# Down-projection of a two-layer decoder trunk: partial sums over all feature pairs kept in PSUM, product by product

## The chip, the cores and the metric

The kernel runs on one core of a Trainium2 chip. The metric is the device time of one execution in microseconds (us), lower is better. A core has five instruction streams that the text names: PE (TensorE matmuls; its weight loads are listed as PEld), DVE (VectorE), ACT (ScalarE), POOL (GpSimd) and SP (SyncE, which here only issues DMAs). Each stream runs its instructions in the order in which the scheduler has written them; an instruction that waits holds up what stands behind it on its engine.

## The reference

The program is one inference step of a decoder trunk of two layers, over 1024 prompt tokens and 8 x 8 sample tokens, so 1088 token rows of 1024 numbers. Each layer is a mixer (a gated delta rule in layer 0, dilated window attention in layer 1) followed by a SwiGLU feed-forward; between the layers one key/value projection is made. The part that the change touches is the feed-forward with its residual:

```python
def swiglu(x, w_in, w_out):
    gate, up = jnp.split(x @ w_in, 2, axis=-1)
    return (jax.nn.silu(gate) * up) @ w_out
...
        x = x + rms_norm(swiglu(rms_norm(x, norms[layer, 2]), ffn_w_in[layer], ffn_w_out[layer]), norms[layer, 3])
```

The inner width is 2816, which is 22 feature tiles of 128 (NF = 22), or 11 pairs of them. All numbers are float32.

## The kernel before

Tokens come in nine tiles (TILES): 0 to 7 of 128 prompt tokens each and tile 8 with the 64 sample tokens. A float32 matmul is made of three matmuls of a reduced format: every operand is split into a rounded part (hi, made by ACT with a copy) and the rest (lo, made by a subtraction x - hi on DVE or POOL), and hi x hi, lo x hi and hi x lo are added up in PSUM.

Each layer runs `ffn_in` and then `ffn_out`. `ffn_in` is the up-projection: 11 blocks of two feature tiles, each a fast 2 x 2 matrix multiplication with seven products in place of eight. Its weight sums are made by POOL (L294), split by ACT and DVE (L303, L304), its gate products are made by POOL (L323), and at a block's end one POOL DMA (L357) writes the block's activations, a tile called `wide`, to a DRAM scratch `gd` of [22, 128, 1088].

`ffn_out` is the down-projection, again with seven products on a 2 x 2 split: tokens in two halves of 512 (tiles 0 to 3 and 4 to 7), output columns in two halves of 512, and the feature tiles of a pair as even and odd. It works through blocks of two feature pairs, five blocks, and within a block through the products j = 0 to 6. Each feature's activations (`graw`, 544 KB) and weights (`wraw`, 512 KB) are loaded by SP (L410, L412). For each product the token sums `s` and weight sums `t` are made on POOL (L428 to L439), both operands are split into `ga` and `wa` (hi at L379 on ACT, lo at L380 on DVE and POOL in the turn DVE, POOL, DVE), four token tiles of six matmuls of 512 columns each run on PE (L394), and each result is added from PSUM to an SBUF sum by DVE (L398; copied by ACT in the first block). Tile 8 is multiplied plainly with `gdec`, a split of its 64 columns. The 11th pair is done as a plain product, merged with the residuals tile by tile: `residual` squares on ACT, takes the root on POOL (L153, L154), scales and adds on DVE (L217, L218) and POOL (L216, L219). In layer 0 the same loop goes on, for each tile, to `scale`, `turn` (eight transposes, L187) and the key/value projection `kv_proj` (24 matmuls, L1289).

A scheduler sets the order of instructions on each engine. What it may hoist is limited by the ring sizes of the tile pools: `ga` and `wa` have four buffers each, `graw` and `wraw` eight.

Of the kernel before, what the change touches and what calls it, by code (L numbers as in the profile page):

```python
# [13 lines left out]
F32 = mybir.dt.float32  # L14
F32R = mybir.dt.float32r
# [7 lines left out]
P = 128  # L23
# [13 lines left out]
HALF = T // 2  # L37
# [42 lines left out]
class Net:  # L80
# [185 lines left out]
    def ffn_in(self, w_in, gd):  # L266
# [7 lines left out]
        with ExitStack() as es:  # L274
# [62 lines left out]
            for blk in range(NF // 2):  # L337
# [19 lines left out]
                nc.gpsimd.dma_start(gd[2 * blk:2 * blk + 2].rearrange("f p t -> p f t"), y.rearrange("p f x t -> p f (x t)"))  # L357

    def ffn_out(self, gd, w_out, grow_idx, xin, xout, after):
# [3 lines left out]
        nc, tc = self.nc, self.tc  # L363
        with ExitStack() as es:
# [3 lines left out]
            halves = cycle((nc.vector, nc.gpsimd, nc.vector))  # L368

            def main(raw, half):  # L370
                return bass.AP(tensor=raw.tensor, offset=raw.offset + half * HALF, ap=[list(raw.ap[0]), [HC[1][0], 2], [1, 256]])

            def split(pool, tag, x, bufs):
                t = pool.tile([P, 2, 512], F32R, tag=tag, name=tag, bufs=bufs)
                if len(x.shape) == 3:
                    hi, lo = (t[:, i].rearrange("p (c t) -> p c t", c=2) for i in range(2))
                else:
                    hi, lo = t[:, 0], t[:, 1]
                nc.scalar.activation(hi, x, AF.Copy)  # L379
                next(halves).tensor_sub(lo, x, hi)  # L380
                return t

            def decode(raw):
                t = fy.tile([P, 2 * SD], F32R, tag="gdec", name="gdec", bufs=4)
                hi, lo = (t[:, x * SD:x * SD + SD].rearrange("p (x t) -> p x t", x=2) for x in range(2))
                x = raw[:, :, 256:288]
                nc.scalar.activation(hi, x, AF.Copy)
                nc.vector.tensor_sub(lo, x, hi)
                return t

            def accumulate(out, seq, first=False):
                ps = self.bank("mm")
                for i, (a, b) in enumerate(seq):
                    nc.tensor.matmul(ps, a, b, start=i == 0, stop=i == len(seq) - 1)  # L394
                if first:
                    nc.scalar.activation(out, ps, AF.Copy)
                else:
                    nc.vector.tensor_add(out, out, ps)  # L398
# [1460 lines left out]
```

## Time and profile before

| | us |
|---|---|
| time before, median of 3 runs | 3381.87 (3379.75 to 3384.51) |
| the profiled execution's own time | 3379.78 |
| span of its profile | 3378.1 |
| first ffn_out (layer 0, with the key/value projection) | 1388.3 to 1740.3 |
| second ffn_out (layer 1), which ends the program | 3071.5 to 3378.1 |
| PE busy over the span | 3121.5 (92%) |
| DVE, ACT, POOL busy over the span | 2252.6 (67%), 1541.1 (46%), 1408.5 (42%) |

The profile gives busy time by engine for any stretch (windows), groups of equal instructions with their mean length and with what ended the idle time before them, and a timeline by engine, in which `[2.07 <-POOL ga L380]` behind a row says that the engine stood idle for 2.07 us before it and that a POOL instruction of line 380, which wrote a tile `ga`, ended the wait. The granted clock is the share of TensorE's full speed: 1.00 is 2.4 GHz and 0.50 is 1.2 GHz.

### The profile page before, as it was taken

The page shows a single profiled execution, that of the slowest core. Times are in us where ns is not written, and L with a number is a line of the kernel's source. Part 1 is how long each engine was busy: PE and PEld are TensorE (multiplying, and loading weights), DVE is VectorE, ACT ScalarE, POOL GpSimd, SP SyncE. Part 2 cuts the span into 40 slices and gives each one's busy share as a digit, 9 for nine tenths or more (in the row PEclk, how much of TensorE's full clock was granted, in tenths as well). Part 3 has the DMA queues.
Part 4 walks back from the last instruction along what each step waited for, and adds up shares of the span by engine and source line. Part 5 has one row for each costly group of instructions (what it writes and reads, how often), then busy time and mean ns, then how long its engine had stood idle before and what let it go on. Part 6 is the DMA issues. An engine that isn't in the chain of part 4 may idle for free.

```text
span 3378.1 us, 54405 instructions
## 1 busy us (share of the span) xinstructions
PE 3121.5 (92%) x20096; PEld 2847.5 (84%) x20096; DVE 2252.6 (67%) x4661; ACT 1541.1 (46%) x3783; POOL 1408.5 (42%) x1350
## 2 busy tenths in 40 slices
PE   7899999999899999899899999998898999998986
PEld 7888888888799999777689888887686999997774
DVE  5667777624665555688856777677656655556898
ACT  5445555434433333443457677766334333334333
POOL 3333333343454444487631213120123544445877
PEclk9999999999999999999899999999889999999998
DMA  4233333345322221421251112112442222214113
GB/s 143 92 99 100 111 106 99 98 124 183 109 75 75 77 76 63 149 91 65 96 158 47 32 54 60 32 47 68 157 125 97 77 77 77 77 65 168 67 62 113
DMA packets 248839, 311.80 MB, mean 92 GB/s; under 512 B 33058, under 2 KB 204306, under 8 KB 248572
## 3 DMA queue, kind: packets, MB, share of 16 engines
q1 hardware_dynamic: 240572, 276.20, 25.9%
q0 software_dynamic: 7856, 31.56, 2.3%
q8 instruction: 159, 2.61, 0.3%
q14 instruction: 108, 0.88, 0.1%
q10 hardware_dynamic: 144, 0.56, 0.0%
HBM read 227.91 MB, written 80.36 MB: 91 GB/s over the span
## 4 chain that ended last, share of the span: by engine, by line
PE 63%; DVE 14%; POOL 8%; ACT 6%; issue 6%; DMA 3%; SPq 0%; POOLq 0%; ACTq 0%; DVEq 0%
PE mm L355 27%; PE mm L394 6%; PE mm L764 5%; PE mm L1346 5%; PE mm L567 4%; PE B L1054 2%; PE mm L1289 1%; DVE yc L811 1%; ACT s L1437 1%; PE sc L1431 1%; PE o L1469 1%; DVE wa L380 1%; PE A L987 1%; PE tr L1450 1%; DVE qs L1357 1%
## 5 line engine op out<-in xcount | busy, mean ns | idle before, releaser
L394 PE MATMUL mm<-wa,ga 128*128 128x512 f32 x1872 | 472.6, 410 | 65.3 <-DVE wa L380 23.6
L394 PEld LDWEIGHTS mm<-wa,ga 128*128 128x128 f32 x1872 | 364.5, 197 | 167.2 <-DVE wa L380 34.1
L764 PE MATMUL mm<-h_hi,w 128*128 128x352 f32 (+1 forms) x1536 | 440.4, 345 | 10.3 <-ACT xr L801 8.1
L1346 PE MATMUL mm<-h_hi,w 128*128 128x352 f32 (+1 forms) x1152 | 354.4, 342 | 0.0
L764 PEld LDWEIGHTS mm<-h_hi,w 128*128 128x128 f32 x1536 | 280.1, 191 | 22.1 <-ACT xr L801 9.0
L323 POOL TENSOR_TENSOR wide<-wide,v 128x288 f32<-128x288 f32 (+1 forms) x176 | 162.4, 936 | 244.5 <-DVE v L322 244.5
L764 PE MATMUL mm<-h_lo,w 128*128 128x352 f32 (+1 forms) x768 | 257.6, 335 | 0.0
L304 DVE TENSOR_TENSOR s<-w,s 128x512 fp32r<-128x512 f32 x132 | 165.1, 1252 | 128.9 <-ACT s L303 128.6
L303 ACT ACTIVATE s<-t 128x512 fp32r<-128x512 f32 x176 | 111.1, 632 | 288.0 <-PE mm L355 277.6
L294 POOL TENSOR_TENSOR t<-w 128x512 f32<-128x512 f32 x88 | 114.6, 1304 | 299.0 <-issue 159.6
L1346 PEld LDWEIGHTS mm<-h_hi,w 128*128 128x128 f32 x1152 | 212.3, 189 | 1.6
L1437 ACT ACTIVATE s<-s,stat 128x128 f32<-128x128 f32 (+1 forms) x384 | 169.4, 442 | 93.4 <-DVE stat L1435 91.1
L145 POOL TENSOR_TENSOR w<-raw,w 128x1024 fp32r<-128x1024 f32 x38 | 100.5, 2645 | 240.8 <-ACT w L142 181.4
L1346 PE MATMUL mm<-h_lo,w 128*128 128x352 f32 (+1 forms) x576 | 189.3, 329 | 0.0
L567 PE MATMUL mm<-mw_hi,o_hl 128*128 128x512 f32 x544 | 177.3, 403 | 3.7 <-ACT o_hl L555 3.7
L1454 DVE TENSOR_TENSOR pl<-tr,ph 128x256 fp32r<-128x256 f32 (+1 forms) x192 | 104.6, 545 | 106.7 <-ACT ph L1453 105.7
L304 DVE TENSOR_TENSOR s<-t,s 128x512 fp32r<-128x512 f32 x176 | 131.6, 749 | 39.7 <-ACT s L303 39.4
L355 PE MATMUL mm<-b0h,s 128*128 128x256 f32 (+1 forms) x704 | 144.5, 292 | 12.2 <-ACT s L303 9.6
L811 DVE SCALAR_TENSOR_TENSOR yc<-xr,convw,yc 128x1112 f32<-128x1112 f32 x72 | 115.4, 1603 | 52.7 <-ACT yc L809 52.6
L764 PEld LDWEIGHTS mm<-h_lo,w 128*128 128x128 f32 x768 | 147.3, 192 | 1.9 <-issue 0.9
L355 PE MATMUL mm<-b6h,s 128*128 128x256 f32 (+1 forms) x704 | 142.9, 292 | 5.1 <-ACT b6h L190 5.1
L355 PE MATMUL mm<-b1h,s 128*128 128x256 f32 (+1 forms) x704 | 142.9, 291 | 4.9 <-ACT y_mix L570 4.9
(487 smaller groups left out, 9445.1 us busy)
## 6 DMA issues: line engine op xcount, KB each, us to landing
w<-in_ffn_w_in_dram SPq DMA_DIRECT2D x88, 512.0 KB
gd<-wide POOLq DMA_DIRECT2D x22, 1088.0 KB, 5.0
graw<-gd SPq DMA_DIRECT2D x44, 544.0 KB
wraw<-in_ffn_w_out_dram SPq DMA_DIRECT2D x44, 512.0 KB
raw<-in_a_w_in_dram SPq DMA_DIRECT2D x32, 512.0 KB
qkv<-f SPq DMA_DIRECT2D x24, 544.0 KB
xo<-x SPq DMA_DIRECT2D x24, 512.0 KB
raw<-in_b_w_q_dram SPq DMA_DIRECT2D x24, 512.0 KB
```

Source lines behind the costliest of these rows:

```text
L294: op(t, x, y)
L303: nc.scalar.activation(out[j][:, 0], x, AF.Copy)
L304: nc.vector.tensor_sub(out[j][:, 1], x, out[j][:, 0])
L323: nc.gpsimd.tensor_tensor(out, out, v, op=ALU.mult)
L355: nc.tensor.matmul(ps[:, :HC[c][1]], u, v, start=z == 0, stop=z == 11)
L394: nc.tensor.matmul(ps, a, b, start=i == 0, stop=i == len(seq) - 1)
L567: nc.tensor.matmul(ps, a, b[:, k], start=k == 0 and i == 0, stop=k == KD - 1 and i == len(seq) - 1)
L764: nc.tensor.matmul(ps[:, :n], a[:, k, :], b[:, k, n0:n0 + n], start=i_ == 0, stop=i_ == 23)
L811: nc.vector.scalar_tensor_tensor(yc, xr[:, j:j + CW], w(j), yc, op0=ALU.mult, op1=ALU.add)
L1346: nc.tensor.matmul(ps[:, :n], a[:, k, :], b[:, k, n0:n0 + n], start=i == 0, stop=i == 23)
L1437: nc.scalar.activation(s[:, a, :n], s[:, a, :n], AF.Exp, bias=m, scale=-1.0, accum_out=stat[:, 1, a, b:b + 1])
L1454: nc.vector.tensor_sub(pl[:, :nk], pt[:, :nk], ph[:, :nk])
```

## The change

`ffn_in` now also makes the four token sums of the down-projection, s1, s2, s4 and s3, on POOL (four operations of 128 x 512 per block) and writes, for each pair of features, seven ready left operands of 512 columns to a DRAM scratch `gs` of [11, 128, 7, 512]; `gd` keeps the 64 sample columns only. That makes six POOL DMAs per block in place of one.

`ffn_out` runs the products j on the outside and the 11 pairs p on the inside: 77 steps of 12 matmuls, with each of the four token tiles summed in one PSUM bank over the 11 pairs and read out once per product. The weights of all pairs stay in SBUF (`we` and `wo`, 11 tiles each); the weight sums are made in place by POOL, one per step of the products 1 to 4 (L428 of the new kernel). In those products lo is made in the turn DVE, DVE, DVE, POOL, in the others in the turn DVE, POOL, so that there `ga` goes to DVE and `wa` to POOL (L391). `ga` and `wa` have three buffers. The residuals of the tiles 0, 1, 2, 3 and 8 are merged into the products 5 and 6; those of the tiles 4 to 7, and in layer 0 all nine `kv_proj`, come after the products. The diff, with the removed body of `ffn_out` (printed above) left out:

```diff
-    def ffn_in(self, w_in, gd):
+    def ffn_in(self, w_in, gs, gd):
...
                         evac(i, c, x[c], k, ps, y)
-                nc.gpsimd.dma_start(gd[2 * blk:2 * blk + 2].rearrange("f p t -> p f t"), y.rearrange("p f x t -> p f (x t)"))
+                a11, a21, a12, a22 = (bass.AP(tensor=x.tensor, offset=x.offset, ap=[list(x.ap[0]), [HC[1][0], 2], [1, 256]])
+                                      for x in (y[:, f, half] for f in range(2) for half in range(2)))
+                s = self.wide()[:, :2048].rearrange("p (j t) -> p j t", j=4)
+                s1, s2, s4, s3 = (s[:, j].rearrange("p (c t) -> p c t", c=2) for j in range(4))
+                for op, out, u, v in ((nc.gpsimd.tensor_add, s1, a21, a22), (nc.gpsimd.tensor_sub, s2, s1, a11),
+                                      (nc.gpsimd.tensor_sub, s4, a12, s2), (nc.gpsimd.tensor_sub, s3, a11, a21)):
+                    op(out, u, v)
+                for j, x in ((0, a11), (1, a12), (6, a22)):
+                    nc.gpsimd.dma_start(gs[blk, :, j].rearrange("p (c t) -> p c t", c=2), x)
+                nc.gpsimd.dma_start(gs[blk, :, 2:6], s)
+                for f in range(2):
+                    nc.gpsimd.dma_start(gd[2 * blk + f].rearrange("p (x t) -> p x t", x=2), y[:, f, :, 256:288])
...
-    def ffn_out(self, gd, w_out, grow_idx, xin, xout, after):
+    def ffn_out(self, gs, gd, w_out, grow_idx, xin, xout, after):
...
+        NP = NF // 2
+            sw, se = ExitStack(), ExitStack()
+            fw, fe = self.pool(sw, "ffwo"), self.pool(se, "ffwe")
+            wo = [fw.tile([P, D], F32, name=f"wo{p}") for p in range(NP)]
+            we = [fe.tile([P, D], F32, name=f"we{p}") for p in range(NP)]
+            lohalf = {True: cycle((nc.vector, nc.vector, nc.vector, nc.gpsimd)), False: cycle((nc.vector, nc.gpsimd))}
+            def split(pool, tag, x, bufs, busy):
+                nc.scalar.activation(t[:, 0], x, AF.Copy)
+                next(lohalf[busy]).tensor_sub(t[:, 1], x, t[:, 0])
+                return t
+            def decode(f0, n):
+                raw = fe.tile([P, n, SD], F32, tag="draw", name="draw", bufs=1)
+                nc.sync.dma_start(raw, gd[f0:f0 + n].rearrange("f p t -> p f t"))
+                t = fe.tile([P, n, 2, SD], F32R, name=f"gdec{f0}")
+                nc.scalar.activation(t[:, :, 0], raw, AF.Copy)
+                nc.vector.tensor_sub(t[:, :, 1], raw, t[:, :, 0])
+                return [t[:, f].rearrange("p x t -> p (x t)") for f in range(n)]
+            L, R = slice(0, 512), slice(512, D)
+            dec = []
+            order = [(j, p) for j in range(7) for p in range(NP)]
+            graws = {}
+            def load(j, p):
+                g = (fe if j < 5 else fo).tile([P, 512], F32, tag=f"graw{int(j < 5)}", name="graw", bufs=8 if j < 5 else 4)
+                nc.sync.dma_start(g, gs[p, :, j])
+                graws[j, p] = g
+                for k, w, f, c in ((0, we, 0, L), (1, wo, 1, L), (1, we, 0, R), (2, wo, 1, R)):
+                    if k == j:
+                        nc.sync.dma_start(w[p][:, c], w_out[(2 * p + f) * P:(2 * p + f + 1) * P, c])
+                if j == 0 and p in (3, 10):
+                    dec.extend(decode(*((0, 12) if p == 3 else (12, 10))))
+            def operands(j, p):
+                e, o = we[p], wo[p]
+                busy = 0 < j < 5
+                g = split(fo, "ga", graws.pop((j, p)), 3, busy)
+                w = split(fo, "wa", (e[:, L], o[:, L], e[:, L], e[:, L], o[:, R], o[:, R], o[:, L])[j], 3, busy)
+                x = split(fe, "wx", e[:, R], 2, busy) if j == 4 else None
+                if busy:
+                    out, a, b = (None, (e[:, L], e[:, R], e[:, L]), (e[:, L], o[:, R], e[:, L]), (o[:, L], e[:, L], o[:, L]), (o[:, R], o[:, R], e[:, R]))[j]
+                    nc.gpsimd.tensor_sub(out, a, b)
+                return g, w, x
+            acc = {}
+            def step(j, p, g, w, x):
+                for i in range(4):
+                    if p == 0:
+                        acc[i] = self.bank("acc")
+                    c = slice(i * P, i * P + P)
+                    for n, (u, v) in enumerate(((0, 0), (1, 0), (0, 1))):
+                        nc.tensor.matmul(acc[i], g[:, u, c], w[:, v], start=p == 0 and n == 0, stop=p == NP - 1 and n == 2)
+                    if p == NP - 1:
+                        evac(j, i, acc[i], *(y[i][:, k] for k in range(4)))
+                if j in (0, 1, 4):
+                    if p == 0 and j != 1:
+                        acc["d"] = self.bank("yd")
+                    todo = [(dec[2 * p + int(j > 0)], w[:, v]) for v in range(2)] + ([(dec[2 * p], x[:, v]) for v in range(2)] if j == 4 else [])
+                    for n, (a, b) in enumerate(todo):
+                        nc.tensor.matmul(acc["d"], a, b, start=p == 0 and j != 1 and n == 0, stop=p == NP - 1 and j > 0 and n == len(todo) - 1)
+                    if p == NP - 1 and j > 0:
+                        nc.scalar.activation(yd[:, R if j == 4 else L], acc["d"], AF.Copy)
+            def evac(j, i, ps, c11, c12, c21, c22):
+                if j in (0, 2):
+                    nc.scalar.activation(c22 if j else c21, ps, AF.Copy)
+                elif j == 1:
+                    nc.vector.tensor_add(c11, c21, ps)
+                elif j == 4:
+                    nc.vector.tensor_add(c12, c22, ps)
+                    nc.gpsimd.tensor_add(c12, c12, c21)
+                elif j == 6:
+                    nc.vector.tensor_sub(c21, c21, ps)
+                    nc.vector.tensor_add(c21, c21, ps)
+                    if j == 5:
+                        nc.gpsimd.tensor_add(c22, c22, c21)
+            def steps(order, ahead):
+                todo = list(order)
+                for s in todo[:ahead]:
+                    load(*s)
+                held = operands(*todo[0])
+                for n, s in enumerate(todo):
+                    for z in todo[n + ahead:n + ahead + 1]:
+                        load(*z)
+                    now, held = held, operands(*todo[n + 1]) if n + 1 < len(todo) else None
+                    step(*s, *now)
+                    yield 1 / len(todo)
+            self.banks(acc=4, mm=3, yd=1)
+            for _ in steps(order[:5 * NP], 6):
+                pass
+            se.close()
+            self.banks(acc=4, mm=2, sm=2)
+            pre, post = after()
+            self.rpool = self.jpool = self.pool(es, "fft", "right")
+            self.rb = 4
+            grow = self.gain_rows(*grow_idx, self.rpool)
+            live = {}
+            def start(tt, _):
+                if tt == 8:
+                    t = self.rpool.tile([P, D], F32, tag="raw", name="ysum", bufs=self.rb)
+                    nc.scalar.activation(t[:SD], yd[SD:], AF.Copy)
+                    nc.vector.tensor_add(yd[:SD], yd[:SD], t[:SD])
+                    v = yd[:SD]
+                    k = tt // 4 * 2
+                    v = y[tt % 4][:, k:k + 2].rearrange("p a b -> p (a b)")
+                return self.residual(tt, v, xin(tt), xout(tt), grow)
+            def rounds(r0, r1):
+                stages = (start, *pre)
+                for r in range(r0, r1):
+                    for s in range(len(stages)):
+                        if 0 <= r - s < NT:
+                            tt = TILES[r - s]
+                            live[tt] = stages[s](tt, live.get(tt))
+                    yield 1 / (r1 - r0)
+            merge(steps(order[5 * NP:], 3), rounds(0, 5))
+            sw.close()
+            last = list(TILES)
+            stage = post(es) if post else None
+            for _ in rounds(5, NT + len(pre)):
+                if stage:
+                    stage(last.pop(0))
+            for tt in last if stage else ():
+                stage(tt)
...
+        gs, gd = dram("gs", [NF // 2, P, 7, 512]), dram("gd", [NF, P, SD])
+                    self.ffn_in(a["ffn_w_in"][0], gs, gd)
+            def after():
+                self.h_pool(eh, side="right")
+                def proj(es):
+                    self.wpool, self.wb = self.pool(es, "ffkv"), 4
+                    return lambda tt: self.kv_proj(tt, h2, w, kv, kv_outs)
+                return into(None, h2), proj
+            self.ffn_out(gs, gd, a["ffn_w_out"][0], (0, 3), x1, x2, after)
+                self.ffn_in(a["ffn_w_in"][1], gs, gd)
+        self.ffn_out(gs, gd, a["ffn_w_out"][1], (1, 3), x3, x4, lambda: ((), None))
```

The scheduler's order shows three places where instructions stand in another row than before.

The first is SP's queue at the start of the first `ffn_out`. Before, the loads of activations and weights of the first block stood there in turn:

```order
L410 DMA graw<-gd 128x1088
L412 DMA wraw<-in_ffn_w_out_dram 128x1024
L410 DMA graw<-gd 128x1088
L412 DMA wraw<-in_ffn_w_out_dram 128x1024
L410 DMA graw<-gd 128x1088
```

Now four loads of `graw` that belong to later pairs stand first, then ten loads of left halves of `wo`, and behind them the `graw` and the `we` of the first step:

```order
L411 DMA graw<-gs 128x512 x4
L415 DMA wo_14734<-in_ffn_w_out_dram 128x512
L415 DMA wo_14735<-in_ffn_w_out_dram 128x512
...
L415 DMA wo_14743<-in_ffn_w_out_dram 128x512
L411 DMA graw<-gs 128x512
L415 DMA we_14745<-in_ffn_w_out_dram 128x512
L411 DMA graw<-gs 128x512
L415 DMA we_14746<-in_ffn_w_out_dram 128x512
```

The loads of `wo`, which the product 1 reads first, moved ahead of those that the product 0 begins with; the first `wo` lies in memory that the operand `s6` of `ffn_in` holds until the last matmul of `ffn_in`.

The second place is POOL's row at the seam of the two functions. Before, one lo (`wa`) stood ahead of the last gate product and the block's DMA:

```order
L323 TENSOR_TENSOR wide<-wide,v 128x288
L380 TENSOR_TENSOR wa<-wraw,wa 128x512
L323 TENSOR_TENSOR wide<-wide,v 128x256
L357 DMA gd<-wide 128x2x1088
L428 TENSOR_TENSOR s<-graw 128x512
```

Now the block's DMAs, the four sums and the DMA of the sums stand ahead of the first lo:

```order
L323 TENSOR_TENSOR wide<-wide,v 128x288
L368 DMA gd<-wide 256x1x32
L323 TENSOR_TENSOR wide<-wide,v 128x256
L363 TENSOR_TENSOR wide<-wide 128x512 x4
L366 DMA gs<-wide 128x2048
L391 TENSOR_TENSOR wa<-we_14745,wa 128x512
L391 TENSOR_TENSOR wa<-we_14746,wa 128x512
```

The first lo of the new `ffn_out` moved behind all POOL work of `ffn_in`.

The third place is POOL in the product 2 of the first `ffn_out`. Before, a steady block had this row (sums of tokens and weights between lo parts):

```order
L380 TENSOR_TENSOR ga<-s,ga 128x512
L431 TENSOR_TENSOR s<-s,graw 128x512 x2
L434 TENSOR_TENSOR s<-graw,s 128x512
L432 TENSOR_TENSOR t<-wraw,t 128x512 x2
L380 TENSOR_TENSOR wa<-t,wa 128x512
L439 TENSOR_TENSOR t<-t,wraw 128x512
L434 TENSOR_TENSOR s<-graw,s 128x512
L439 TENSOR_TENSOR t<-t,wraw 128x512
```

Now the row begins as follows, and the pattern goes on to the 11th pair:

```order
L391 TENSOR_TENSOR wa<-we_14745,wa 128x512
L428 TENSOR_TENSOR we_14745<-wo_14734,we_14745 128x512
L428 TENSOR_TENSOR wo_14734<-we_14745,wo_14734 128x512
L428 TENSOR_TENSOR we_14746<-wo_14735,we_14746 128x512
L391 TENSOR_TENSOR wa<-we_14747,wa 128x512
L428 TENSOR_TENSOR wo_14735<-we_14746,wo_14735 128x512
L428 TENSOR_TENSOR we_14747<-wo_14736,we_14747 128x512
L428 TENSOR_TENSOR wo_14736<-we_14747,wo_14736 128x512
L428 TENSOR_TENSOR we_14748<-wo_14737,we_14748 128x512
L428 TENSOR_TENSOR wo_14737<-we_14748,wo_14737 128x512
L391 TENSOR_TENSOR wa<-we_14749,wa 128x512
```

Two weight sums per pair stand here, that of the product 2 (into `we`) and that of the product 3 (into `wo`), which moved up out of the product 3: 22 sums and 6 lo parts on POOL for 11 steps.

## Rows read from the trace of the kernel before

**Rows 1.** Windows: PE, PEld, DVE, ACT, POOL busy, clock, DMA, GB/s.
```profile
1300.00:1388.30 88.30, 88.30 (x703) 88.30 (x702) 46.78 (x82) 24.68 (x49) 33.30 (x33) 1.00 0.23 82
1388.30:1412.00 23.70, 15.15 (x51) 10.78 (x51) 20.38 (x19) 10.18 (x22) 15.77 (x13) 0.84 0.74 294
1600.00:1700.00 100.00, 82.48 (x321) 64.43 (x322) 88.65 (x103) 43.28 (x83) 69.48 (x67) 0.85 0.32 105
1388.30:1740.30 352.00, 315.21 (x1315) 249.52 (x1315) 284.77 (x348) 155.69 (x306) 250.96 (x200) 0.93 0.34 115
3071.50:3378.10 306.60, 252.57 (x1025) 196.66 (x1023) 260.78 (x306) 122.77 (x236) 238.58 (x178) 0.93 0.29 103
```

**Rows 2.** PE's timeline, a steady block of the first ffn_out.
```profile
1458.03 12.08 PE L394 MATMUL mm<-wa,ga 128*128 128x512 f32 x50 [0.51 <-DVE wa L380]
1472.18 6.42 PE L394 MATMUL mm<-wa,ga 128*128 128x512 f32 x20 [2.07 <-POOL ga L380]
...
1480.25 21.92 PE L394 MATMUL mm<-wa,ga 128*128 128x512 f32 x96
1502.01 1.98 PE L394 MATMUL mm<-wa,gdec 128*128 128x512 f32 x8
...
1504.95 1.43 PE L394 MATMUL mm<-wa,ga 128*128 128x512 f32 x5 [0.51 <-DVE wa L380]
```

**Rows 3.** PE's timeline just after the first ffn_out has begun.
```profile
1397.73 1.65 PE L394 MATMUL mm<-wa,ga 128*128 128x512 f32 x3 [5.04 <-DVE ga L380]
```

**Rows 4.** Window behind that stall, columns as in rows 1.
```profile
1400.00:1404.00 4.00, 3.85 (x9) 3.07 (x10) 2.13 (x5) 2.23 (x5) 0.00 (x0) 0.50 1.03 422
```

**Rows 5.** Groups by form, first ffn_out: busy us, mean ns, idle before.
```profile
L398 DVE TENSOR_TENSOR y<-y,mm 128x512 f32<-128x512 f32 x77 | 50.3, 679 | 14.4 <-PE mm L394 14.3
L380 DVE TENSOR_TENSOR ga<-graw,ga 128x512 fp32r<-128x512 f32 x27 | 35.8, 1331 | 6.9 <-ACT ga L379 6.9
...
L379 ACT ACTIVATE ga<-graw 128x512 fp32r<-128x512 f32 x43 | 26.9, 626 | 64.2 <-PE mm L394 57.3 <-POOL graw L436 6.1
```

**Rows 6.** DVE's timeline there: start us, us, instruction.
```profile
1391.46 5.62 DVE L388 TENSOR_TENSOR gdec<-graw,gdec 128x64 fp32r<-128x64 f32 x1
...
1400.02 0.68 DVE L380 TENSOR_TENSOR wx<-wraw,wx 128x512 fp32r<-128x512 f32 x1
...
1411.55 1.76 DVE L432 TENSOR_TENSOR t<-wraw,t 128x512 f32<-128x512 f32 x1
```

**Rows 7.** POOL's timeline, the same stretch.
```profile
1409.35 1.72 POOL L380 TENSOR_TENSOR wa<-wraw,wa 128x512 fp32r<-128x512 f32 x1
```

**Rows 8.** SP's timeline at the end of the first ffn_in.
```profile
1373.43 0.34 SPq L410 DMA_DIRECT2D graw<-gd  x1
...
1385.90 0.44 SPq L412 DMA_DIRECT2D wraw<-in_ffn_w_out_dram  x1
```

**Rows 9.** POOL's timeline, one block of the first ffn_in.
```profile
1221.78 0.76 POOL L357 DMA_DIRECT2D gd<-wide  x1 [0.30 <-POOL wide L323]
1222.56 1.31 POOL L294 TENSOR_TENSOR t<-w 128x512 f32<-128x512 f32 x1
...
1235.76 1.30 POOL L294 TENSOR_TENSOR t<-w 128x512 f32<-128x512 f32 x1 [10.65 <-DVE s L304]
...
1264.15 0.76 POOL L357 DMA_DIRECT2D gd<-wide  x1 [0.30 <-POOL wide L323]
```

**Rows 10.** PE's timeline, its last entry.
```profile
3355.08 4.84 PE L394 MATMUL mm<-wa,ga 128*128 128x512 f32 x18 [1.57 <-DVE y L398]
```

**Rows 11.** POOL's timeline, the last four instructions of the span.
```profile
3370.25 0.19 POOL L153 TENSOR_SCALAR rstd<-ss 128x1 f32<-128x1 f32 x1
3370.52 0.55 POOL L154 TENSOR_TENSOR rstd<-rstd,mhalf 128x1 f32<-128x1 f32 x1
3371.69 1.01 POOL L216 TENSOR_TENSOR y<-y,grow 128x256 f32<-128x256 f32 x1 [0.62 <-ACT y L215]
3372.78 1.32 POOL L219 TENSOR_TENSOR y<-y,xo 128x256 f32<-128x256 f32 x1
```

More of the change, by code (lines that the diff above doesn't have):

```diff
@@ L367, in ffn_out @@
             yd = fy.tile([P, D], F32, name="yd")
[L368 to L373, printed above, removed]
-                t = pool.tile([P, 2, 512], F32R, tag=tag, name=tag, bufs=bufs)
-                if len(x.shape) == 3:
-                    hi, lo = (t[:, i].rearrange("p (c t) -> p c t", c=2) for i in range(2))
-                else:
[L378 to L396, printed above, removed]
-                else:
-                    nc.vector.tensor_add(out, out, ps)
@@ L497, in ffn_out @@
-            self.wpool, self.rpool = self.pool(es, "ffw"), self.pool(es, "fft")
-            self.jpool = self.rpool
-            self.rb, self.wb = 4, 4
-            self.banks(mm=4, sm=4)
-            grow = self.gain_rows(*grow_idx, self.rpool)
-            after = after()
-            def last(tt, _):
-                half, i = tt // 4, tt % 4
-                for nh in range(2):
-                    if tt == 8:
-                        accumulate(yd[:, nh * 512:nh * 512 + 512], [(g, w[:, v]) for g, w in zip(ops[2], ops[1][nh]) for v in range(2)])
-                    else:
-                        accumulate(y[i][:, 2 * half + nh], [x for g, w in zip(ops[0][half], ops[1][nh]) for x in product(g, w, slice(i * P, i * P + P))])
-                if tt < 8:
-                    return y[i][:, 2 * half:2 * half + 2].rearrange("p a b -> p (a b)")
-                t = self.rpool.tile([P, D], F32, name="ysum", bufs=1)
-                nc.scalar.activation(t[:SD], yd[SD:], AF.Copy)
-                nc.vector.tensor_add(yd[:SD], yd[:SD], t[:SD])
-                return yd[:SD]
@@ L1779, in run @@
                     self.banks(mm=6, sm=2)
-                    self.ffn_in(a["ffn_w_in"][0], gd)
+                    self.ffn_in(a["ffn_w_in"][0], gs, gd)
             kv = dram("kv", [T, NKV, 3, DH])
@@ L1821, in run @@
                 self.banks(mm=6, sm=2)
-                self.ffn_in(a["ffn_w_in"][1], gd)
-        with ExitStack() as es:
-            self.ffn_out(gd, a["ffn_w_out"][1], (1, 3), x3, x4, tuple)
+                self.ffn_in(a["ffn_w_in"][1], gs, gd)
+        self.ffn_out(gs, gd, a["ffn_w_out"][1], (1, 3), x3, x4, lambda: ((), None))
 @with_exitstack
```

96 lines of the change are left out of this document (removed).

## The prediction

> **What bounds the kernel now.** I read the windows first. In `ffn_in` PE is busy for all of 88.3 us at clock 1.00 and POOL for 33.3 [rows 1]: that stage is bound by PE. The two `ffn_out` are not. The first holds PE for 315 of 352.0 us at a mean clock of 0.93, the second for 253 of 306.6 at 0.93, while DVE is busy for 285 and 261 [rows 1]. So I look there for who is waited for.
>
> The pace of PE unhindered comes from its timeline: 96 matmuls of 512 columns start at 1480.25 and the next entry at 1502.01, 0.2267 us each [rows 2]. A steady block of 184 matmuls would take 41.7 us by that; it takes 46.92 (1458.03 to 1504.95) [rows 2]. One stall of 2.07 us behind a POOL lo is part of the 5.2 lost. The rest is clock, whose price is plainest at the stage's start. There PE stands for 5.04 us [rows 3], and in the window behind it the granted clock is 0.50, the level of 1.2 GHz, and nine matmuls take 4.00 us in place of 2.04 [rows 4]. So a long stall costs itself and about 2 us more. The start as a whole: 51 matmuls, 11.6 us, take 23.7, a loss of 12.1 [rows 1]. The end of the blocks is worse: from 1600 to 1700 PE is busy for 82.5 at clock 0.85, with DVE at 88.7 [rows 1].
>
> Why DVE and POOL are late is seen in single rows. A DVE lo takes 0.68 us when POOL is out of the way, a neighbour 1.76 while POOL's takes 1.72 [rows 6, 7]; alone POOL takes 1.31 for the same 128 x 512 [rows 9]. The mean of the lo of `ga` is 1331 ns, that of the additions from PSUM 679 [rows 5]: the first suffer from POOL, the second do not. One DVE operation of 64 columns even lasted 5.62 us while POOL ran on [rows 6].
>
> **The change part by part.** *PE.* Before, an `ffn_out` had 1024 such matmuls (5 blocks of 168 plus 16, 96 in the last pair, 8 for tile 8). After it has 77 steps of 12 and 88 for tile 8: 1012, or 229.4 us. That alone is 2.7 us less. Layer 0 adds 9 x 24 matmuls of `kv_proj`, 49.0 us, and the transposes, which I take at 0.8 us per tile, 7.2 in all (an estimate).
>
> *DVE* loses nearly all additions from PSUM: 77 of 679 ns in the group of `y` before 1700 [rows 5], and by the loops 48 more into `m`, 85 us, besides the weight sums of the first block. They held DVE, so lo parts queued behind them; that is the gain, and it comes out as fewer stalls, so I count the stalls that stay. *POOL* has in the steps 33 lo parts in the products 0, 5 and 6, 25 in the others, 44 weight sums and 8 additions: 110 operations, about 140 us at 1.26 to 1.31 alone, against 229 of PE. In the mean it suffices. It is a matter of where they are bunched, and the order shows three bunches.
>
> *Start.* Ten loads of `wo` stand ahead of the first operands and cannot be issued before the end of `ffn_in`; before, the first load went out at 1373.43, some 15 us ahead of that end [rows 8]. Twelve issues at 0.44 us are 5.3 us [rows 8]; their 3.1 MB at the 422 GB/s of a full window [rows 4] are 7.5. Two hi parts at 0.63 [rows 5] and a lo of 1.3 on POOL follow: 10 us at least, 12 with the time a transfer takes to land (1.5, an estimate that no row gives). POOL's own queue is ready by then: a product, the last DMAs at 0.76 plus 0.30 and four sums, 5.2 us, end about 10 us behind the last matmul. With 3 us of half clock: **15** per stage, where 12.1 was lost before. Bounds: 10 and 25.
>
> *Product 2.* 28 POOL operations at 1.26 are 35.3 us; some 16 DVE subtractions that meet them cost POOL 0.46 each (1.72 less 1.26), 7.4 more. PE needs 11 x 12 x 0.2267 = 29.9. With a lead of two steps, 5.4 us, since the rings are three deep: 7.4 late, and with some half clock **10**. Bounds: 0 (the lead covers it) and 29 (all eleven steps at half clock: 11 x 12 x 0.2177 extra). The product 3 then has hardly a POOL operation but its lo, the products 0, 1 and 4 have fewer than PE needs time for (product 0: 22 operations and 16 meetings, about 35 of 35 us).
>
> Here a rule speaks against the change. By the Trainium skill, SBUF — State Buffer, section "Who interferes with whom", DVE with two SBUF inputs and POOL take one port pair as an exclusive lock, and DVE with one SBUF input stays free of it. The trace agrees: 679 ns for the additions, 1331 for the lo. So the additions that go had never used the port, and by a strict lock product 2 would need 35.3 + 16 x 0.68 = 46 us, 4 more than my sum; 8 us over both stages, which lies within the range.
>
> *Products 5 and 6.* Five residuals come into product 5. POOL has 11 lo (13.9), four additions (5.0) and per residual 0.19 + 0.55 + 1.01 + 1.32, about 3.1 [rows 11], 15.4: 34 us, and with 21 DVE subtractions beside it at 0.46 nearly 44, against 29.9. Less 4 of lead, plus 2 of clock: **12**, in layer 0 with the roots of `scale` **14**. The lo of the next step stands in POOL's queue behind roots that wait for ACT's square, so 29 is the upper bound here too, 0 the lower. Product 6 has 11 lo and four additions: enough time. The seams between the products (reading four banks, four POOL additions ahead of a lo) take **4** per stage.
>
> *Tail.* PE's last matmul began its run at 3355.08 and ended at 3359.9, and the span ends at 3378.1 [rows 1, 10]: 18.2 us for residuals that follow one another. Now four residuals remain behind the last matmul. POOL holds them for 4 x 3.1 = 12.4, the first root can start as PE stops, and from the last addition's end, 3374.1 [rows 11], to the span's end lie 4.0: **16.5**. In layer 0 `kv_proj` fills PE there instead; 2 us for its start.
>
> *`ffn_in`.* Per block of 42.4 us (1221.78 to 1264.15) POOL gets four sums at 1.31 and five DMAs at 0.76 + 0.30: 10.5 us [rows 9]. It was busy for 38% [rows 1], and waited for 10.65 us ahead of a weight sum until DVE released its buffer [rows 9]; the operands made from it are used a product round later. Cost nothing: the cover is that wait. If it were gone, PE would wait for split weights, up to 10 us a block.
>
> *The sum.* Second stage: 229.4 + 15 + 10 + 12 + 4 + 16.5 = 286.9 against 306.6, 19.7 less. First: 229.4 + 49.0 + 7.2 + 15 + 10 + 14 + 4 + 2 = 330.6 against 352.0, 21.4 less. Together 41 of the profiled execution's 3379.8: **3339 us**. That execution lies 2.1 below the median, which I leave uncorrected.
>
> **The rivals.** (a) *PE sets the pace nearly throughout*: the rings' lead takes up the bunches of the products 2 and 5. Then 10 + 12 + 10 + 14 = 46 more go, **3293**. For it speaks that POOL's total is far below PE's; against it, a block before stalled on one POOL lo though POOL had free time [rows 2]. (b) *`ffn_in` pays*: the 10.5 us of new POOL work delay the weight sums. At 1 us of wait per block, 22 us over 22 blocks, **3361**; at 1.9 us a block the gain is gone. Against it: the 10.65 us of idle time. (c) *Slower: the starved steps run at half clock.* If the 22 steps of the products 2 and 5 keep PE at 0.50 throughout, each takes 12 x 0.444 = 5.3 us in place of the 3.8 I count, 33 per stage, 66 in all: **3405**. It decides when some 60% of those steps are so. For it: the window of 100 us in which PE was busy for 82% stood at 0.85 [rows 1], and at a stage's start four microseconds ran at 0.50 [rows 4]. Against it: at 5.3 us a step POOL and DVE, which need about 3.9, catch up, PE is busy throughout, and in the steady block it was back at 0.2267 us a matmul 8 us behind the stall [rows 2]. (d) The change doesn't do what it says: DVE's relief doesn't reach PE because each lo still waits for POOL; that is between (b) and (c), within 7 us of no change.
>
> **How the numbers follow.** My sum 0.50, (a) 0.15, (b) 0.14, (d) 0.07, (c) 0.14. No change means within 0.2%, 7 us, about what a measurement can tell here. Faster: the first three, 0.79; same: 0.07; slower: 0.14. The range leaves out (c) and half of what lies at (a)'s far side: **3295 to 3380**.
>
> **What would show it.** Right: a first wait of some 12 us at each stage's start behind SP's `wo` loads; waits on POOL's weight sums or `wa` in product 2; waits in product 5; a full clock in the products 1, 3, 4 and 6; DVE far below 285 us in the first stage; `ffn_in` with PE at 100%. Wrong: idle PE in `ffn_in`, half clock over whole products, or a start above 25 us.

## The result and the profile after

The changed kernel takes 3356.3 us (median of four runs, 3349.1 to 3358.2) against 3383.2 for the kernel before, a ratio of 0.9915 with a 95% interval of 0.9894 to 0.9935: some 0.85% faster. The forecast was 3339 us, the range 3295 to 3380. The profiled execution of the changed kernel is the fastest of its four (3349.1), so I compare stages. A stage `ffn_out` is counted from the last matmul of `ffn_in` to the first of the next part (or the end of the span).

| | before | after | forecast |
|---|---|---|---|
| first ffn_out, us | 352.0 | 337.6 | 330.6 |
| second ffn_out, us | 306.6 | 293.8 | 286.9 |

Together 27.2 us less, and the medians differ by 26.9. The rest by which this one span is shorter lies in parts that the change leaves alone; the last matmul of the first `ffn_in` ended between 1382.1 and 1394.8 us in profiles of programs that are the same up to there in all that PE does. The stages repeat far better (338.2 and 294.0 in a second profile), and the experiments are read by them.

Windows of the changed kernel, columns as in [rows 1]. The first is the end of `ffn_in`, then the wait at the start of `ffn_out`, the products 0 to 4 (each from its first matmul to the next one's), product 5 with the transposes in it, product 6 with the wait ahead of it, and the two stages:

```profile
1300.00:1385.90 85.90, 85.90 (x683) 85.84 (x682) 46.14 (x80) 22.77 (x46) 50.23 (x51) 1.00 0.25 82
1385.90:1399.00 13.10, 0.15 (x2) 0.00 (x0) 1.11 (x2) 1.26 (x2) 8.30 (x9) 0.69 0.94 309
1399.02:1437.71 38.69, 38.18 (x154) 30.43 (x155) 16.80 (x16) 18.74 (x32) 28.37 (x20) 0.93 0.93 313
1437.71:1473.85 36.14, 35.22 (x155) 28.83 (x154) 15.69 (x20) 13.18 (x24) 17.02 (x13) 1.00 0.52 162
1473.85:1512.92 39.07, 32.72 (x134) 25.61 (x132) 23.98 (x18) 14.48 (x26) 36.93 (x25) 0.96 0.24 68
1512.92:1542.84 29.92, 29.92 (x134) 24.68 (x132) 12.49 (x18) 13.29 (x24) 9.93 (x8) 1.00 0.34 97
1542.84:1582.78 39.94, 39.94 (x178) 33.06 (x177) 30.47 (x32) 18.10 (x33) 29.86 (x20) 1.00 0.12 34
1582.78:1628.89 46.11, 35.99 (x141) 26.97 (x139) 32.82 (x27) 25.71 (x48) 40.18 (x41) 0.93 0.47 155
1628.89:1666.26 37.37, 33.65 (x150) 27.83 (x151) 21.11 (x28) 17.11 (x31) 20.07 (x15) 0.95 0.40 120
1385.90:1723.60 337.70, 300.46 (x1302) 241.24 (x1301) 180.01 (x192) 148.37 (x275) 220.43 (x186) 0.96 0.49 153
3053.50:3347.40 293.90, 242.62 (x1013) 194.08 (x1012) 157.94 (x150) 115.79 (x205) 202.16 (x154) 0.93 0.45 144
```

The reader sees the three places at which PE waits: 13.1 us with hardly a matmul; product 2 (1473.9 to 1512.9), PE 32.7 of 39.1 with POOL at 36.9; product 5 (1582.8 to 1628.9), PE 36.0 of 46.1 with POOL at 40.2. The products 1, 3 and 4 run at clock 1.00. DVE, 285 us before [rows 1], is down to 180. `ffn_in` still holds PE for all of its time though POOL there went from 38% to 58%.

The start, as SP's timeline shows it, and behind it PE's first entry:

```profile
1373.98 5.17 SPq L411 DMA_DIRECT2D graw<-gs  x4
1386.08 4.87 SPq L415 DMA_DIRECT2D wo<-in_ffn_w_out_dram  x10
1391.24 0.33 SPq L411 DMA_DIRECT2D graw<-gs  x1
1391.87 0.33 SPq L415 DMA_DIRECT2D we<-in_ffn_w_out_dram  x1
```

```profile
1399.02 9.74 PE L439 MATMUL acc<-wa,ga 128*128 128x512 f32 x29 [12.97 <-ACT wa L390]
```

Four early loads, then nothing until the last matmul of `ffn_in` (1386.0), ten loads of `wo`, and only then the operands of the first step.

POOL in product 2, and PE's entry that waited for its last row here:

```profile
1481.37 1.62 POOL L428 TENSOR_TENSOR wo<-we,wo 128x512 f32<-128x512 f32 x1
1482.95 1.77 POOL L428 TENSOR_TENSOR we<-wo,we 128x512 f32<-128x512 f32 x1
1484.80 1.59 POOL L428 TENSOR_TENSOR wo<-we,wo 128x512 f32<-128x512 f32 x1
1486.36 1.70 POOL L391 TENSOR_TENSOR wa<-we,wa 128x512 fp32r<-128x512 f32 x1
```

```profile
1488.12 5.73 PE L439 MATMUL acc<-wa,ga 128*128 128x512 f32 x24 [2.77 <-POOL wa L391]
```

This lo stands in POOL's row behind the weight sums, among them those of product 3 (into `wo`), and PE waits 2.77 us for it.

### The profile page after: what moved, and what is told of

It reads as the page before. It is cut to its first block, busy times and chain, and to the rows that moved or that the text cites. A ratio compares the mean times of both kernels' runs of the same rounds, so it can differ in the third digit from the quotient of the medians.

```text
span 3347.4 us, 54525 instructions
## 1 busy us (share of the span) xinstructions
PE 3090.6 (92%) x20072; PEld 2829.6 (85%) x20072; DVE 2093.5 (63%) x4347; ACT 1522.6 (45%) x3717; POOL 1513.9 (45%) x1488
## 4 chain that ended last, share of the span: by engine, by line
PE 64%; DVE 10%; POOL 9%; ACT 6%; issue 6%; DMA 5%; SPq 0%; POOLq 0%; ACTq 0%; DVEq 0%
PE mm L355 27%; PE acc L439 7%; PE mm L764 5%; PE mm L1346 5%; PE mm L567 4%; PE B L1054 2%; DVE yc L811 1%; ACT s L1437 1%; POOL we L428 1%; POOL wa L391 1%; PE o L1469 1%; PE sc L1431 1%; PE A L987 1%; PE mm L1289 1%; DVE qs L1357 1%
## 5 line engine op out<-in xcount | busy, mean ns | idle before, releaser
L439 PE MATMUL acc<-wa,ga 128*128 128x512 f32 x1848 | 455.9, 402 | 66.3 <-ACT wa L390 27.1
L439 PEld LDWEIGHTS acc<-wa,ga 128*128 128x128 f32 x1848 | 354.9, 194 | 154.9 <-POOL wa L391 36.5
L391 DVE TENSOR_TENSOR ga<-graw,ga 128x512 fp32r<-128x512 f32 x150 | 151.5, 1011 | 216.3 <-ACT ga L390 213.4
L304 DVE TENSOR_TENSOR s<-w,s 128x512 fp32r<-128x512 f32 x132 | 188.3, 1428 | 101.5 <-ACT s L303 101.3
L323 POOL TENSOR_TENSOR wide<-wide,v 128x288 f32<-128x288 f32 (+1 forms) x176 | 149.4, 849 | 199.3 <-DVE v L322 198.9
L390 ACT ACTIVATE ga<-graw 128x512 fp32r<-128x512 f32 x154 | 97.1, 630 | 303.4 <-PE acc L439 233.9
L304 DVE TENSOR_TENSOR s<-t,s 128x512 fp32r<-128x512 f32 x176 | 161.0, 916 | 45.9 <-ACT s L303 45.6
```

What stands on the lines that cost most here:

```text
L304: nc.vector.tensor_sub(out[j][:, 1], x, out[j][:, 0])
L323: nc.gpsimd.tensor_tensor(out, out, v, op=ALU.mult)
L391: next(lohalf[busy]).tensor_sub(t[:, 1], x, t[:, 0])
L439: nc.tensor.matmul(acc[i], g[:, u, c], w[:, v], start=p == 0 and n == 0, stop=p == NP - 1 and n == 2)
```

## The experiments

Stage sums (first and second `ffn_out` together) are 658.6 us before and 631.4 after. "Less" and "more" below are differences of such sums; each run has one profile.

**1. SP's queue at the start** (`e1_gate`). A tiny DVE copy out of each first step's `graw` into the weight tiles holds the later loads back:

```diff
+                if j == 0:
+                    nc.vector.tensor_copy(wo[p][:, 0:D:512], graws[j, p][:, 0:2])
+                    nc.vector.tensor_copy(we[p][:, 512:513], graws[j, p][:, 0:1])
```

> The loads of wo and of the right halves of we are held back behind the loads of product 0 (each waits for a tiny DVE copy out of that step's graw). First theory (SP's queue makes the start late): the first wait of PE in each ffn_out falls from 13.0 us to about 10, where POOL's four sums, their DMA and the first lo become the last to arrive; some 3 us per stage and 5 to 6 in all. Rival (the transfers themselves take that long to land): the wait stays at 13 and the time does not move.

Measured: stages 334.4 and 289.3, 7.7 less than after; 3342.6 us, ratio 0.9871 (0.9856 to 0.9886). PE's first entries:

```profile
1387.05 0.39 PE L442 MATMUL acc<-wa,ga 128*128 128x512 f32 x1
1389.11 0.50 PE L442 MATMUL acc<-wa,ga 128*128 128x512 f32 x1 [1.67 <-DVE ga L391]
1398.39 4.21 PE L442 MATMUL acc<-wa,ga 128*128 128x512 f32 x9 [8.78 <-POOL wa L391]
```

The first operands are there at once, and the wait falls to 10.5 us in two parts, the second for the lo that stands behind POOL's last sums. The first theory holds, with its number for the wait; the gain of 7.7 us is above its 5 to 6.

**2. All lo of the products 1 to 4 on DVE** (`e2_lo_dve`).

```diff
-            lohalf = {True: cycle((nc.vector, nc.vector, nc.vector, nc.gpsimd)), False: cycle((nc.vector, nc.gpsimd))}
+            lohalf = {True: cycle((nc.vector,)), False: cycle((nc.vector, nc.gpsimd))}
```

> In the products 1 to 4 every lo is made by DVE, none by POOL; POOL keeps the weight sums. First theory (lo parts stand in POOL's queue behind weight sums that the scheduler has moved up from product 3): the three stalls of product 2 go, its 38 us fall to about 32, the products 1, 3 and 4 stay, some 10 us less in all. Rival (DVE and POOL slow each other down in any split of the work): product 2 stays above 36 us, product 4, with 33 lo parts, grows.

Measured: 328.8 and 287.0, 15.6 less; 3339.7 us, ratio 0.9865 (0.9846 to 0.9885). The three stalls of product 2 are gone. It takes 33.6 us, in the first stage with five waits of 0.36 to 0.39 us behind DVE; a sixth, in the first step of product 3, is the only other one in the products 1 to 4. The window of product 2, two of PE's entries, and three of POOL, which has the sums alone, while DVE is never idle:

```profile
1479.35:1512.95 33.60, 31.71 (x133) 24.31 (x132) 33.60 (x23) 14.58 (x26) 31.17 (x19) 1.00 0.27 77
```

```profile
1496.95 3.04 PE L439 MATMUL acc<-wa,ga 128*128 128x512 f32 x12 [0.38 <-DVE wa L391]
1500.35 3.02 PE L439 MATMUL acc<-wa,ga 128*128 128x512 f32 x12 [0.36 <-DVE wa L391]
```

```profile
1481.07 1.68 POOL L428 TENSOR_TENSOR we<-wo,we 128x512 f32<-128x512 f32 x1 [3.62 <-DVE wa L391]
1482.83 1.62 POOL L428 TENSOR_TENSOR wo<-we,wo 128x512 f32<-128x512 f32 x1
1484.41 1.74 POOL L428 TENSOR_TENSOR we<-wo,we 128x512 f32<-128x512 f32 x1
```

The first theory's number was 32. What keeps it from there is the rival in small: each POOL operation beside a DVE lo takes 1.6 to 1.7, and a step has two lo on DVE and two sums on POOL, so it takes 3.40 us (1496.95 to 1500.35) against 2.72 of PE. The clock is 1.00 over the whole product.

**3. Residuals unmerged in the code** (`e3_unmerged`): `merge(steps(...), rounds(0, 5))` written as the steps and then the rounds.

> The residuals of the tiles 0, 1, 2, 3 and 8 come after the products 5 and 6 instead of within them. First theory (residuals in product 5 hold up its lo parts): product 5 falls from 46 us to about 31 in both stages; the first stage gains about 8 us, since kv_proj covers the residuals later, the second about nothing, since five residuals of some 3 us join its tail; about 8 us less in all. Rival (the merging hides the residuals well and the 16 us lost in product 5 come from the clock or from the seam): product 5 stays above 40 us, and the time grows by 15 to 30 us.

Measured: 345.4 and 295.4, 9.4 more than after; ratio 0.9925 (0.9905 to 0.9946), the waits of product 5 as they were. This tells nothing on merging: POOL's row kept the residuals between the lo parts of product 5, since the scheduler moves up whatever is ready. Experiment 8 repeats it with a real hold.

**4. PSUM sums undone** (`e4_dve_sums`).

```diff
-                    if p == 0:
+                    if p % 2 == 0:
                         acc[i] = self.bank("acc")
...
-                        nc.tensor.matmul(acc[i], g[:, u, c], w[:, v], start=p == 0 and n == 0, stop=p == NP - 1 and n == 2)
+                        nc.tensor.matmul(acc[i], g[:, u, c], w[:, v], start=p % 2 == 0 and n == 0, stop=(p % 2 or p == NP - 1) and n == 2)
...
-            self.banks(acc=4, mm=3, yd=1)
+            self.banks(acc=7, yd=1)
```

The edit also gives the sums seven PSUM banks in place of four in the products 0 to 4 (the products 5 and 6 keep four).

> PSUM sums only two pairs at a time, as the kernel before did, and DVE adds each result to SBUF: 132 more DVE additions of 0.68 us per stage, all else as in the changed kernel. First theory (the additions held DVE, and lo parts behind them came late): stalls behind DVE come back, 10 to 20 us per stage, 20 to 40 in all, which is most of the gain. Rival (the gain comes from resident weights and ready token sums, DVE being busy for only 180 of 338 us): within 6 us of the changed kernel.

Measured: 337.3 and 291.9; 3350.3 us, ratio 0.9898 (0.9884 to 0.9913). The windows of the two stages, those of the products 0 to 4 and 5 to 6 of the first stage, and a wait in product 5:

```profile
1394.50:1731.90 337.40, 298.97 (x1302) 237.36 (x1302) 258.38 (x332) 148.15 (x275) 221.09 (x186) 0.97 0.49 153
3062.90:3354.80 291.90, 242.08 (x1013) 192.90 (x1012) 228.77 (x290) 115.66 (x205) 200.67 (x154) 0.93 0.45 145
1407.82:1591.39 183.57, 174.83 (x748) 141.78 (x749) 153.55 (x202) 77.11 (x136) 123.44 (x83) 0.98 0.43 134
1591.39:1673.10 81.71, 68.33 (x294) 52.71 (x293) 74.86 (x89) 42.93 (x79) 59.22 (x56) 0.98 0.42 134
```

```profile
1599.47 3.76 PE L439 MATMUL acc<-wa,ga 128*128 128x512 f32 x14 [2.44 <-DVE y L466]
```

DVE has 332 operations in the first stage against 192, 140 more (the expectation says 132), and is busy for 258 us against 180, nearly the 285 of the kernel before. The products 0 to 4 take 183.6 us; in the changed kernel they take 183.8 (1399.02 to 1582.78). In the products 5 and 6 PE now waits behind the additions themselves (2.44 us at 1599.47), while waits behind lo parts go: the two products take 81.7 us, and 83.5 in the changed kernel (1582.78 to 1666.26). With four banks in the products 0 to 4 the additions might have held PE there too; no run shows that. My theory on the cause of the gain, lo parts behind the additions, falls here, and the rival's number holds. The next three runs ask what the cause is: theory A, POOL's token sums; theory B, DVE's additions.

**5. The kernel before without DVE's additions** in the blocks 2 to 4 (`e6_before_no_adds`): `accumulate` leaves out its `tensor_add` there.

> The kernel before, without DVE's additions from PSUM in the blocks 2, 3 and 4 (the products of these blocks are left out of the sum). Theory A (POOL's token sums, ahead of the lo parts that wait for them, set the pace of a block): a steady block stays at 46.9 us, with the 2.07 us stall behind POOL's ga, the first ffn_out within 4 us of 352. Theory B (DVE's additions held up the lo parts): a steady block falls to 42 to 43 us, the stages by 10 us or more each.

Measured: 345.3 and 300.8, 12.5 less than before; ratio 0.9973 (0.9957 to 0.9988), 6.4 us between the medians. A steady block, PE's entries at its start, behind POOL's `ga`, and at the next one's start:

```profile
1458.70 10.96 PE L394 MATMUL mm<-wa,ga 128*128 128x512 f32 x47 [0.73 <-DVE wa L380]
1470.08 4.87 PE L394 MATMUL mm<-wa,ga 128*128 128x512 f32 x20 [0.42 <-POOL ga L380]
...
1504.78 17.11 PE L394 MATMUL mm<-wa,ga 128*128 128x512 f32 x67 [0.73 <-DVE wa L380]
```

46.08 us in place of 46.92 [rows 2]: 84 additions fewer are worth some 6 us a stage, less than theory B's 10 and a little more than A's 4. Theory A had the 2.07 us stall stay, and it fell to 0.42; other waits, behind DVE's and POOL's `wa`, took its place, so the block nearly kept its length.

**6. The kernel before without POOL's token sums** (`e7_before_no_token_sums`).

```diff
-                    add(s, a21, a22)
-                    yield ga(s), wa(t)
-                    sub(s, s, a11)
+                    yield ga(a21), wa(t)
...
-                    yield ga(s), wa(t)
-                    sub(s, a12, s)
-                    yield ga(s), wa(b22), split(fx, "wx", b12, 2)
-                    sub(a21, a11, a21)
+                    yield ga(a11), wa(t)
+                    yield ga(a12), wa(b22), split(fx, "wx", b12, 2)
```

> The kernel before, without POOL's four token sums per pair (the products 2 to 5 take an unsummed part of the tokens as their left operand); DVE's additions stay. Theory A (the token sums on POOL set the pace): the 2.07 us stall behind POOL's ga goes, a steady block falls from 46.9 to about 42 us, each stage by 10 to 20 us. Theory B (DVE's additions set it): the block stays above 45 us.

Measured: 321.4 and 276.8, 60.4 less than before; 3314.0 us, ratio 0.9802 (0.9775 to 0.9829). A steady block (the same place in two blocks):

```profile
1422.34 21.92 PE L394 MATMUL mm<-wa,ga 128*128 128x512 f32 x96
...
1464.14 21.92 PE L394 MATMUL mm<-wa,ga 128*128 128x512 f32 x96
```

41.80 us: 184 matmuls at 0.2267 and nothing lost. Theory A holds by far: 30 us a stage came, where I had put 10 to 20 on it.

**7. The sums' cost put back into the changed kernel** (`e5_pool_sums_back`).

```diff
+                if 1 < j < 6:
+                    nc.gpsimd.tensor_add(graws[j, p], graws[j, p], graws[j, p])
```

> The changed kernel with one more POOL operation of 128 x 512 between load and split in each step of the products 2 to 5 (it doubles that operand), 44 per stage: the token sums' cost on POOL is back where it was, PSUM still sums over all pairs. Theory A: POOL has 39 operations in product 2 for 11 steps and 22 to 35 in the products 3 to 5; product 2 grows from 38 us to 55 or more, the stage by 20 us or more. Theory B: the lead of the rings takes most of it up, the stage grows by less than 8 us.

Measured: 356.1 and 310.8; 3388.7 us, ratio 1.0019 (1.0003 to 1.0036): the whole gain is gone. The two stages, and product 2:

```profile
1390.90:1746.90 356.00, 307.77 (x1300) 246.52 (x1301) 200.61 (x192) 148.58 (x275) 269.80 (x228) 0.93 0.46 145
3076.50:3387.30 310.80, 249.61 (x1012) 197.78 (x1012) 172.87 (x150) 116.32 (x205) 252.45 (x196) 0.91 0.42 136
1478.94:1530.40 51.46, 36.79 (x133) 28.40 (x132) 23.82 (x20) 14.64 (x26) 49.59 (x38) 0.87 0.22 61
```

Product 2 takes 51.5 us with POOL busy for 49.6 of them; theory A had 55 or more. The stages grow by 18.5 and 17.0 us, a little less than its 20 and far more than B's 8. PSUM still sums over all pairs here and the weights still stay in SBUF, and neither keeps the gain. (The kernel before makes 40 token sums per stage, since its 11th pair is plain; here there are 44.)

The stage sums of the runs 6 and 7 beside the two kernels, in us:

| | token sums made on POOL in `ffn_out` | none made there |
|---|---|---|
| loop of the kernel before | 658.6 | 598.2 |
| loop of the changed kernel | 666.9 | 631.4 |

Within each row the token sums are worth 60 and 36 us. Down each column the rest of the change costs time: 8 us with the sums and 33 without. The changed loop brings its own waits (start, product 2, product 5), and takes back about half of the 60 us. A kernel with the loop before and the sums moved to `ffn_in` was not built, so 598.2 leaves out what ready operands would cost there.

**8. Residuals held behind product 6** (`e3b_unmerged_held`): a tiny DVE operation on each of the five reads the last sum of product 6.

```diff
+                if tt in TILES[:5]:
+                    n = tok(tt)[1]
+                    nc.vector.scalar_tensor_tensor(v[:n, 0:1], y[3][:n, 2, 0:1], 0.0, v[:n, 0:1], op0=ALU.mult, op1=ALU.add)
```

> The residuals of the tiles 0, 1, 2, 3 and 8 held back behind product 6 by a tiny DVE operation on each that also reads the last sum of product 6 (without it the scheduler put them back into product 5). First theory (the residuals in product 5 hold up its lo parts): product 5 falls from 46 us to 32 to 34 in both stages; the first stage gains some 8 us, the tail of the second grows by about 15 us and takes the gain away. Rival (the seam and the clock cost product 5 its 16 us): product 5 stays above 40.

Measured: 353.8 and 303.9; ratio 1.0000 (0.9984 to 1.0017). The products 5 and 6 of the first stage, and the tail of the second:

```profile
1587.27:1647.73 60.46, 60.46 (x265) 49.23 (x263) 20.83 (x27) 22.87 (x40) 36.76 (x27) 1.00 0.30 91
3340.80:3386.40 45.60, 0.03 (x1) 0.00 (x0) 25.54 (x26) 15.00 (x28) 30.93 (x36) 0.55 0.44 150
```

Both products run without a stall, product 5 in 29.9 us, so the residuals did cause its 16 us. But the tail of the second stage is 45.6 us in place of 18.6: five residuals cost 27 there, 5.4 each and not 3.1. In the first stage the same residuals leave PE idle ahead of `kv_proj` (first wait 11.6 us). Merging pays, by 26 us over both stages; I had expected the first stage to be some 8 us faster without it.

**9. Residuals spread over both products** (`e8_spread`): the same tiny operation, but reading the left operand of the step beside which the residual is written down (`latest[0]`, set to `now[0]` after each step).

> The five residuals within the products 5 and 6 are spread over them: each waits, by a tiny DVE operation on it, for the left operand of the step beside which it is written down; before, the scheduler had put all five into product 5. First theory (bunching): product 5 falls from 46 to about 40 us, product 6 takes the rest in its free time, 5 us less per stage, 10 in all. Rival (each residual costs the same wherever it stands, by the lo parts behind it): what product 5 gains product 6 loses, within 3 us of the changed kernel.

Measured: 333.5 and 289.4, 8.5 less; 3346.4 us, ratio 0.9897 (0.9875 to 0.9918). From its first matmul to that of product 6, product 5 takes 36.4 us in the first stage and 36.9 in the second (49.8 and 46.8 in the changed kernel); product 6 takes 39.5 and 37.2 (33.7 and 31.0). Product 6 takes back about half, and the first theory holds.

**10. All three together** (`e9_all`), with the lo parts of the first three steps on DVE (what the expectation calls the eighth is number 9 here):

```diff
+                early = nc.vector if j == 0 and p < 3 else None
```

> Loads of the first steps ahead (as in the first experiment), the first three steps' lo parts on DVE so that they don't stand behind POOL's sums, all lo parts of the products 1 to 4 on DVE (as in the second), residuals spread (as in the eighth). First theory (three bunches, independent of each other): start 6 us less per stage, product 2 some 7, products 5 and 6 some 5; 18 us per stage, 36 in all, near 3320 us. Rival (with one stall gone the next one takes its place): less than 22 us in all.

Measured: 317.3 and 271.5, 42.6 less than after; 3317.5 us (3314.0 to 3320.1), ratio 0.9814 (0.9796 to 0.9833). This version beats both kernels. Its stages:

```profile
1388.10:1705.40 317.30, 300.74 (x1301) 240.49 (x1300) 215.24 (x246) 146.41 (x273) 187.66 (x159) 0.97 0.51 159
3043.80:3315.30 271.50, 239.64 (x1013) 191.66 (x1011) 193.91 (x204) 114.33 (x203) 168.90 (x127) 0.95 0.47 152
```

The single gains, 7.7 + 15.6 + 8.5 = 31.8, add up, and 10.8 us come on top. They came with the early lo parts, which no run has alone: the waits at the first stage's start are 1.67 and 1.10 us here, 10.5 together in experiment 1. The rival falls.

**11. The changed kernel again** (`after_again`), beside the last two:

> The changed kernel once more, beside the two others: both theories expect the first ffn_out at 337.6 us, the second at 293.8, and 25 to 30 us less than the kernel before.

Measured: 338.2 and 294.0; 3359.3 us, ratio 0.9933 (0.9908 to 0.9958), 20.7 us between the medians.

## Why the prediction was right, and where it was not

*Direction and size.* Faster, as forecast; 27 us where 41 were forecast. The places that stay were named before the run and are the ones found: the start, product 2, product 5, in the sizes of the next lines.

*The sum.* First stage, lost against PE's own 285.6: 52.0 us, forecast 45. Start 13.0 of wait and 3 of half clock in product 0, 16 (forecast 15). Product 1 one, product 3 none (0). Product 2 39.1 against 29.9, 9 (10). Product 5 46.1 against 29.9, 16.2 (14). The seam to product 6, which I had within 4 for all seams, alone is a wait of 3.7 us behind DVE and 2 us of lower clock, some 6. Around `kv_proj` 4 (2). Second stage: PE's run from its first to its last matmul takes 262.0 against 229.4, and with the start's 13.2 that is 45.8 lost (forecast 41); the tail 18.6 (16.5). So the terms that were too small are product 5 with the seam behind it, and the tail: each rests on the residual, which I priced by POOL's 3.1 us alone, while DVE's `ga` waits behind its scaling and additions too (3.41 us once in product 5). The 1.5 us for a transfer to land, in the start's term, had no row behind it; in the trace of the kernel before, a DMA of 512 KB lands 3.0 us after its issue (median of four, `x<-y_mix`), of which its bytes take 1.2 at the 422 GB/s of [rows 4].

*The step that failed* is the cause: "They held DVE, so lo parts queued behind them; that is the gain". Experiment 4 brings 140 additions per stage back and the stages take no longer, and in the kernel before 84 of them were worth 6 us a stage. What gained is the token sums leaving POOL: 30 us a stage in the kernel before (experiment 6), and with their cost put back the change is worth nothing (7). I had read the clue, a 2.07 us stall behind a POOL `ga` in each block [rows 2], and put it down as part of the loss without asking what stood ahead of that `ga` (at 1470.42) on POOL:

```profile
1464.35 1.30 POOL L434 TENSOR_TENSOR s<-graw,s 128x512 f32<-128x512 f32 x1
1465.59 1.80 POOL L439 TENSOR_TENSOR t<-t,wraw 128x512 f32<-128x512 f32 x1
1467.35 1.74 POOL L380 TENSOR_TENSOR ga<-s,ga 128x512 fp32r<-128x512 f32 x1
1469.17 1.28 POOL L428 TENSOR_TENSOR s<-graw 128x512 f32<-128x512 f32 x1
1470.42 1.71 POOL L380 TENSOR_TENSOR ga<-s,ga 128x512 fp32r<-128x512 f32 x1
```

The sum that it splits was ready at 1465.65. A weight sum, another lo and a token sum for a later product then kept POOL busy until it began. The experiments 6 and 7 move both POOL's time and one link of the chain sum, split, matmul; which of the two counts more is not shown.

The sum of the prediction did not rest on the cause, since it counted the stalls that stay. It took for granted that the old stalls would go, and they went for another reason than the one it gave; in that part it was luck that it came out near.

*`ffn_in` at no cost*: right. PE is busy for all of the window ahead of the stage with POOL at 58%, and from the first stage's end to the second's start pass 1329.9 us where 1331.2 passed before; rival (b) falls. *Rival (c)*, half clock over whole products: the clock was 0.96 in product 2 and 0.93 in product 5; it falls. *Rival (a)* falls too: the lead did not cover the bunches. *Rival (d)* named the engine that mattered, since lo parts did wait for POOL, but the token sums left POOL with the same change, and with 27 us it falls by its time.

*The rule on the shared port*: additions from PSUM cost POOL nothing, in experiment 4 too (POOL 221 us in the first stage with them, 220 without). This is as the Trainium skill says (SBUF — State Buffer, section "Who interferes with whom"): DVE and POOL contend when DVE reads two operands from SBUF, not when it reads one. By its strict lock a step of experiment 2 would cost two times 0.68 + 1.26, 3.9 us, an estimate from that rule. Measured are 3.40, so a lo on DVE and a sum on POOL overlap a little, and the measurement decides. (The 1.76 us row of [rows 6] is a weight sum on DVE, not a lo; the reading stands, since the mean of the lo was 1331 ns [rows 5].)

## What to carry to other kernels

Additions from PSUM on an engine that has time cost little: here 140 per stage put back left the stage as long as it was, and 84 taken out of the kernel before gave 6 us a stage. Look instead for what stands on an engine ahead of the operand that the next matmul waits for, here sums and lo parts on POOL. Work that a stage bound by PE can hide (here 44 sums in `ffn_in`) can be moved there. A change of several parts is worth taking apart: here one part gave the gain and the rest took about half of it back. And what is written down late may be scheduled early: loads for a later product and sums for the next one came to stand ahead of the operands that were due, and an operation of one or two columns that ties such work to the right moment won 7.7 and 8.5 us at two places.

## What the runs showed that I had not expected

A residual alone in the tail costs 5.4 us and not the 3.1 of its longest engine; within PE's work its cost is 3.2 (16.2 us for five). And not every wait costs clock. In experiment 2, product 2 has five waits of 0.36 to 0.39 us and the granted clock is 1.00. In the changed kernel the mean of product 2 is 0.96, but of its three stalls (2.77, 1.63 and 1.95 us) only the third is followed by a lower clock:

```profile
1488.10:1490.10 2.00, 1.98 (x9) 1.65 (x10) 0.00 (x0) 0.00 (x0) 1.88 (x2) 1.00 0.40 118
1495.50:1497.50 2.00, 2.00 (x9) 1.66 (x10) 0.47 (x1) 0.00 (x0) 1.92 (x2) 1.00 0.11 25
1503.20:1505.20 2.00, 2.00 (x6) 1.57 (x7) 0.46 (x1) 0.00 (x0) 1.92 (x2) 0.59 0.14 26
```

Why the third and not the first, which is longer, no run here shows.
